# Rotating 96 images: 32 KB reads into four partitions each, twelve 8 KB slots per side, and one kind of group, in place of two kinds of groups with 8 and 16 KB packets

## The chip, the cores and the metric

The kernel runs on one core of a Trainium2 chip. The metric is the device time of one execution in microseconds (us). "Packet" is one entry of the trace's list of DMA packets; "MB" in my own sums of packets is 1,048,576 bytes.

## The reference

```python
def setup_inputs():
    batch, c, h, w = 32, 3, 256, 256
    return {"x": np.random.randn(batch, c, h, w).astype(np.float32)}

def reference(x):
    return np.rot90(x, k=1, axes=(-2, -1)).astype(np.float32)
```

There are 96 images of 256 x 256 float32 (256 KB each). Nothing is computed. 25.17 MB (decimal) are read, rotated in SBUF by transposes of 32 x 32 blocks on VectorE and by access patterns, and 25.17 MB are written.

## The kernel before

Sixteen images form a group of 4 MB. The first and the last group are of kind 1 (four transfers of 1 MB per side, 8 KB per partition), the four between are of kind 2 (two transfers of 2 MB per side, 16 KB per partition). SyncE issues the loads, ScalarE the stores, and three buffers per side hold three groups.

```python
G = 16
KINDS = [1, 2, 2, 2, 2, 1]
...
in_pool = ctx.enter_context(tc.tile_pool(name="in_pool", bufs=3))
out_pool = ctx.enter_context(tc.tile_pool(name="out_pool", bufs=3))

for g, kind in enumerate(KINDS):
    ...
    if kind == 1:
        ...                       # R = 8
        for s in range(4):
            nc.sync.dma_start(out=Sv[:, s], in_=xv[s])
        for s in range(4):
            ...
            nc.vector.transpose(dst, src)              # 128 x 2048
            nc.scalar.dma_start(out=ov[s], in_=Uv[:, s])
    else:
        ...                       # R = 16
        for b in range(2):
            nc.sync.dma_start(out=Sv[:, b], in_=xv[b])
        ...
        for q in range(R):
            nc.vector.transpose(dst[:, q], src[:, q])  # 128 x 512
        for a in range(2):
            nc.scalar.dma_start(out=ov[a], in_=Uv[:, a])
```

## Time and profile before

| | before |
|---|---|
| time, median | 124.06 us (3 runs, 124.03 to 124.07) |
| span of the profiled run | 122.2 us |
| bytes moved | 50.34 MB (decimal) |
| VectorE busy | 91.3 us (75%) |
| DMA queues q1 and q10 (their records show the loads in q1, the stores in q10) | 49.3% + 48.3% of 16 engines' span |

These are lines of the page of the profiled execution. The two rows of digits are busy tenths in 40 equal slices of the span; the row below them is what the DMA engines moved in each slice.

```profile
span 122.2 us, 170 instructions
DVE 91.3 (75%) x72; POOL 0.2 (0%) x4
...
DVE  0199999007999999999999990799999999092000
...
DMA  3999999999999999999999999999999999999993
GB/s 86 424 421 416 375 432 429 426 410 442 418 440 437 437 434 418 429 434 429 429 429 429 434 429 421 453 410 413 464 413 429 445 416 426 442 429 408 429 429 161
...
q1 hardware_dynamic: 2304, 25.17, 49.3%
q10 hardware_dynamic: 2304, 25.17, 48.3%
...
L65 DVE STREAM_TRANSPOSE U<-S 128x512 f32<-128x512 f32 x64 | 60.5, 1059 | 10.8 <-DMA S<-in_x_dram 7.1
```

The DMA row is at 9 in every slice but the first and the last, while VectorE (DVE) has gaps. The DMA engines bound this kernel.

The view by stretches of time, of the same run, in the middle (columns: stretch in us, its length, VectorE busy and instructions, GpSimd, granted clock, DMA share, GB/s):

```profile
30.00:60.00 30.00, 30.00 (x33) 0.00 (x0) 1.00 1.01 431
60.00:105.00 45.00, 40.12 (x34) 0.00 (x0) 1.00 1.01 430
```

The Trainium skill, "DMA: Bandwidth & Descriptors", section "Where 436 GB/s comes from", gives a ceiling of 16 x 32 B x 850 MHz = 435.2 GB/s. The middle runs within 1.2% of it.

### The profile page before, as it was taken

The page shows a single profiled execution, that of the slowest core. Times are in us where ns is not written, and L with a number is a line of the kernel's source. Part 1 is how long each engine was busy: PE and PEld are TensorE (multiplying, and loading weights), DVE is VectorE, ACT ScalarE, POOL GpSimd, SP SyncE. Part 2 cuts the span into 40 slices and gives each one's busy share as a digit, 9 for nine tenths or more (in the row PEclk, how much of TensorE's full clock was granted, in tenths as well). Part 3 has the DMA queues.
Part 4 walks back from the last instruction along what each step waited for, and adds up shares of the span by engine and source line. Part 5 has one row for each costly group of instructions (what it writes and reads, how often), then busy time and mean ns, then how long its engine had stood idle before and what let it go on. Part 6 is the DMA issues. An engine that isn't in the chain of part 4 may idle for free.

```text
span 122.2 us, 170 instructions
## 1 busy us (share of the span) xinstructions
DVE 91.3 (75%) x72; POOL 0.2 (0%) x4
## 2 busy tenths in 40 slices
DVE  0199999007999999999999990799999999092000
POOL 0000000000000000000000000000000000000000
DMA  3999999999999999999999999999999999999993
GB/s 86 424 421 416 375 432 429 426 410 442 418 440 437 437 434 418 429 434 429 429 429 429 434 429 421 453 410 413 464 413 429 445 416 426 442 429 408 429 429 161
DMA packets 4609, 50.34 MB, mean 412 GB/s; under 512 B 512, under 2 KB 512, under 8 KB 512
## 3 DMA queue, kind: packets, MB, share of 16 engines
q1 hardware_dynamic: 2304, 25.17, 49.3%
q10 hardware_dynamic: 2304, 25.17, 48.3%
q14 instruction: 1, 0.01, 0.0%
HBM read 25.17 MB, written 25.17 MB: 412 GB/s over the span
## 4 chain that ended last, share of the span: by engine, by line
DMA 61%; DVE 27%; issue 1%; SPq 1%
DMA S<-in_x_dram 46%; DVE U L65 24%; DMA out_dram<-U 16%; DVE U L49 3%; SPq L44 1%
## 5 line engine op out<-in xcount | busy, mean ns | idle before, releaser
L65 DVE STREAM_TRANSPOSE U<-S 128x512 f32<-128x512 f32 x64 | 60.5, 1059 | 10.8 <-DMA S<-in_x_dram 7.1
L49 DVE STREAM_TRANSPOSE U<-S 128x2048 f32<-128x2048 f32 x8 | 31.0, 3937 | 8.7 <-DMA S<-in_x_dram 8.7
L82 POOL MEMSET const-bfloat16-1.0<- 128x1 bf16 x1 | 0.1, 101 | 0.0
L82 POOL MEMSET const-uint8-127<- 128x1 uint8 x1 | 0.1, 101 | 0.0
L82 POOL MEMSET const-float32-0.0<- 128x1 f32 x1 | 0.1, 98 | 0.2 <-issue 0.2
L82 POOL MEMSET const-float32-1.0<- 128x1 f32 x1 | 0.1, 98 | 0.0
## 6 DMA issues: line engine op xcount, KB each, us to landing
S<-in_x_dram SPq DMA_DIRECT2D x8, 2048.0 KB, 21.1
out_dram<-U ACTq DMA_DIRECT2D x8, 2048.0 KB, 19.0
S<-in_x_dram SPq DMA_DIRECT2D x8, 1024.0 KB, 16.6
out_dram<-U ACTq DMA_DIRECT2D x8, 1024.0 KB, 16.1
```

The costliest lines, as they stand in the source:

```text
L44: nc.sync.dma_start(out=Sv[:, s], in_=xv[s])
L49: nc.vector.transpose(dst, src)
L65: nc.vector.transpose(dst[:, q], src[:, q])
L82: nc = _bacc.Bacc("TRN2", target_bir_lowering=False, num_devices=1)
```

## The change

The intent: fewer and longer packets on the load side (each read takes 32 KB of DRAM, which lands in four partitions of 8 KB), loads favoured over stores by that length, and one kind of group (8 images, one store of 2 MB in 16 KB packets). The buffers become twelve slots of 1 MB per side, the same 12 MB as before. The first load alone keeps 8 KB packets.

```diff
-    G = 16
-    KINDS = [1, 2, 2, 2, 2, 1]
+    RI = 8
+    FI = RI * W
+    MS = [2] * 12
+    NS, NU = 12, 12
+    FOLD = 32
...
+    xp = xf.rearrange("(n p f) -> n p f", p=P, f=FI)
+    xv = xf.rearrange("(n d f) -> n d f", n=N // 4, d=FOLD)
...
+    def load(dst, src):
+        nc.sync.add_instruction(mybir.InstDMACopy(
+            ...
+            ins=[nc.sync.lower_ap(src, opt=False)],
+            outs=[nc.sync.lower_ap(dst, opt=False)],
+            queue="qSPDynamicHW", mode="Copy"))
...
+        for b in range(m):
+            if n + b < 1:
+                nc.sync.dma_start(out=S[:, b], in_=xp[n + b])
+            else:
+                load(S[:, b], xv[n + b])
...
+            for r in range(RI):
+                nc.vector.transpose(dst[:, r], src[:, r])
...
+        nc.scalar.dma_start(
+            out=ov.rearrange("b (qk f) -> qk b f", f=RO * W), in_=U
+        )
```

More of the change, by code (lines that the diff above doesn't have):

```diff
@@ L20 @@
     P = 128
-    G = 16
-    KINDS = [1, 2, 2, 2, 2, 1]
-    assert len(KINDS) * G == N
-    F = G * H * W // P
-    fp32 = mybir.dt.float32
-    xf = x.rearrange("b c h w -> (b c h w)").rearrange("(g f) -> g f", g=N // G)
-    of = out.rearrange("b c h w -> (b c h w)").rearrange("(g f) -> g f", g=N // G)
-    in_pool = ctx.enter_context(tc.tile_pool(name="in_pool", bufs=3))
-    out_pool = ctx.enter_context(tc.tile_pool(name="out_pool", bufs=3))
-    for g, kind in enumerate(KINDS):
-        S = in_pool.tile([P, F], fp32, name="S")
-        U = out_pool.tile([P, F], fp32, name="U")
-        if kind == 1:
-            R = 8
-            Sv = S.rearrange("p (s f) -> p s f", s=4)
-            Uv = U.rearrange("p (s f) -> p s f", s=4)
-            xv = xf[g].rearrange("(s p f) -> s p f", s=4, p=P)
-            ov = of[g].rearrange("(s p f) -> s p f", s=4, p=P)
-            for s in range(4):
-                nc.sync.dma_start(out=Sv[:, s], in_=xv[s])
-            for s in range(4):
-                src = Sv[:, s].rearrange("p (r k q) -> p q r k", r=R, q=R)[:, ::-1, :, ::-1]
-                dst = Uv[:, s].rearrange("p (q k r) -> p q r k", q=R, r=R)
-                nc.vector.transpose(dst, src)
-                nc.scalar.dma_start(out=ov[s], in_=Uv[:, s])
-        else:
-            R = 16
-            Sv = S.rearrange("p (b f) -> p b f", b=2)
-            Uv = U.rearrange("p (a f) -> p a f", a=2)
-            xv = xf[g].rearrange("(b a qk f) -> b qk a f", b=2, a=2, f=F // 2)
-            ov = of[g].rearrange("(b a qk f) -> a qk b f", b=2, a=2, f=F // 2)
-            for b in range(2):
-                nc.sync.dma_start(out=Sv[:, b], in_=xv[b])
-            src = Sv.rearrange("p b (r k q) -> p q r k b", r=R, q=R)[:, ::-1, :, ::-1]
-            dst = Uv.rearrange("p a (q k r) -> p q r k a", q=R, r=R)
-            for q in range(R):
-                nc.vector.transpose(dst[:, q], src[:, q])
-            for a in range(2):
-                nc.scalar.dma_start(out=ov[a], in_=Uv[:, a])
@@ new lines @@
+    RI = 8
+    FI = RI * W
+    MS = [2] * 12
+    assert 4 * sum(MS) == N
+    NS, NU = 12, 12
+    FOLD = 32
+    fp32 = mybir.dt.float32
+    xf = x.rearrange("b c h w -> (b c h w)")
+    of = out.rearrange("b c h w -> (b c h w)")
+    xp = xf.rearrange("(n p f) -> n p f", p=P, f=FI)
+    xv = xf.rearrange("(n d f) -> n d f", n=N // 4, d=FOLD)
+    S_all = ctx.enter_context(tc.tile_pool(name="S", bufs=1)).tile([P, NS, FI], fp32, name="S_all")
+    U_all = ctx.enter_context(tc.tile_pool(name="U", bufs=1)).tile([P, NU, FI], fp32, name="U_all")
@@ new lines, in load @@
+    def load(dst, src):
+        nc.sync.add_instruction(
+            mybir.InstDMACopy(
+                name=nc.get_next_instruction_name(),
+                engine=mybir.EngineType.SP,
+                ins=[nc.sync.lower_ap(src, opt=False)],
+                outs=[nc.sync.lower_ap(dst, opt=False)],
+                queue="qSPDynamicHW",
+                mode="Copy",
+            )
+        )
+    n = s = u = 0
+    for m in MS:
+        if s + m > NS:
+            s = 0
+        if u + m > NU:
+            u = 0
+        RO = RI * m
+        S = S_all[:, s : s + m]
+        U = U_all[:, u : u + m].rearrange("p m f -> p (m f)")
+        for b in range(m):
[3 more added lines that the diff above has]
+                load(S[:, b], xv[n + b])
+        src = S.rearrange("p b (r k q) -> p r q k b", r=RI, q=RO)[:, :, ::-1, ::-1]
+        dst = U.rearrange("p (q k r) -> p r q k", q=RO, r=RI)
+        if m == 1:
+            nc.vector.transpose(dst, src[:, :, :, :, 0])
+        else:
+            for r in range(RI):
+                nc.vector.transpose(dst[:, r], src[:, r])
+        ov = of.rearrange("(n f) -> n f", f=P * FI)[n : n + m]
+        nc.scalar.dma_start(
+            out=ov.rearrange("b (qk f) -> qk b f", f=RO * W), in_=U
+        )
+        n += m
+        s += m
+        u += m
```

## The prediction

> **What bounds the kernel now.** The 16 DMA engines. 50.33 MB move; the rows by slice show DMA at 9 in all but the first and last slice, the table by stretches gives a DMA share of 1.00 to 1.02 and 424 to 433 GB/s from 15 to 119 us. VectorE is busy 75% (91.3 of 122.2 us) and its waits cost nothing. The packet records give 309 ns for 8 KB and 611 ns for 16 KB, in both directions: a slope of 27.1 bytes/ns per engine (434 GB/s for 16) plus about 7 ns per packet; a completion packet takes 9 ns. The Trainium skill, "DMA: Bandwidth & Descriptors", section "Where 436 GB/s comes from", puts a ceiling at 435; this trace agrees. Per engine: 128 x 309 + 128 x 611 ns + 32 x 9 ns = 118.05 us. The rest of the 122.2 us span: 2.5 us until the first packet, about 1.3 us of slow first packets and of skew between engines, 0.4 us after the last. The time is 1.85 us over the span.
>
> **What the change does.** Bytes are unchanged. Loads become one of 8 KB packets and 23 of 32 KB reads (if a read is one packet: 2 per engine and load, about 1.215 us each, estimated from the slope); the 12 stores of 2 MB keep 16 KB. Per engine: 2.5 + 46 x 1.215 + 96 x 0.611 + 36 x 0.009 = 117.3 us, which is 0.7 us less, all on the critical path. If instead each 8 KB write counts as a packet, 118.3 us, 0.25 us more.
>
> VectorE gets 96 transposes of 512 columns: at 1.059 us, 101.7 us instead of 91.3, off the path as long as it starts near 8 us (after two loads) and is fed. It then ends near 110 us, and the last 2 MB store (4.9 us) must still find a backlog of earlier stores; by my estimate, stepping the packets through both queues, it does, with 3 to 4 us to spare. A transpose over about 1.10 us would show in the time. The two patterns of before cost alike (3.94 us for four times the columns), so I expect 1.06 us.
>
> **Arbitration.** The same page, section "Queues, rings and completion order", says an engine alternates between queues packet by packet. The trace agrees: from 14 to 44 us, 16 KB loads against 8 KB stores, 2 MB loads and 1 MB stores both land every 7.3 us, a 2:1 split. So 32 KB reads against 16 KB stores give the loads two thirds: loads run ahead until slots or semaphores hold them, VectorE is never starved, stores have the backlog for the end. If the unit were the 8 KB write, loads would get one third, VectorE would starve from about 50 us, and some 6 us of DMA idle would stand before the last store: about 129 us.
>
> **Prediction: 123.4 us, range 122.5 to 125.2.** Faster by over 2%: 0.03; within 2%: 0.87; slower by over 2%: 0.10.
>
> **What would show it.** Load packets of 32 KB near 1.21 us; DMA at 9 in all middle slices, about 430 GB/s; 2 MB of loads landing for each 1 MB of stores early on; VectorE busy about 102 us, its waits only early; the chain of waits ending in stores that land back to back about 4.9 us apart; the load queue waiting mostly for stores.
>
> **What would make it wrong.** A 32 KB read off the slope; arbitration by write; [...] transposes slower than 1.10 us; or a gap before the last store. A gain over 2% needs over 434 GB/s, of which nothing here hints.

## More of the kernel before

Most executions of the kernel before lie within 0.3% of each other; verdicts use runs in the undisturbed state.

Look at the fifth slice, 12.2 to 15.3 us: 375 GB/s although the engines are busy.

## The result, and the profile after

The changed kernel takes 124.28 us (median of 4 runs, 124.15 to 124.31); the kernel before took 124.05 us in the same rounds (123.97 to 124.07). The ratio is 1.0018, 95% interval 1.0001 to 1.0036. A second submission of the same kernel (`again`, below) gave 124.32 us against 123.97 us, ratio 1.0026, 1.0007 to 1.0046. A ratio here is the mean time of one kernel's fast runs over that of the other's of the same rounds, so it is not quite the ratio of the medians. Executions over 1.5% slower than the fastest of the same kernel are left out of the means. The change makes the kernel 0.2 to 0.3% slower: both intervals lie just above 1. I had forecast 0.5% faster.

The lines of the page of the changed kernel that answer to those above:

```profile
span 122.5 us, 206 instructions
DVE 94.0 (77%) x96; POOL 0.2 (0%) x4
...
DVE  0039999999999999999949969950799995994000
...
DMA  4999999999999999999999999999899998999992
GB/s 112 498 417 439 417 407 342 364 428 428 428 433 455 455 444 401 455 401 465 436 385 492 385 407 428 449 417 498 364 444 417 439 498 353 428 428 428 428 428 96
...
q1 hardware_dynamic: 1248, 25.17, 49.3%
q10 hardware_dynamic: 1728, 25.17, 48.0%
...
L73 DVE STREAM_TRANSPOSE U_all<-S_all 128x512 f32<-128x512 f32 x96 | 94.0, 1161 | 17.6 <-DMA S_all<-in_x_dram 15.1
```

The load queue has 1248 packets in place of 2304, and yet it takes the same 49.3% of the span. The slow slices are now the seventh and eighth (18.4 to 24.5 us, 342 and 364 GB/s). The same stretches as before, from the view by stretches:

```profile
30.00:60.00 30.00, 30.00 (x32) 0.00 (x0) 1.00 1.02 437
60.00:105.00 45.00, 35.39 (x37) 0.00 (x0) 1.00 1.00 427
```

Over both stretches that is (30 x 437 + 45 x 427) / 75 = 431.0 GB/s, where before had 430.4. Long packets make a short stretch's figure coarse, because a packet is counted where it falls, so I also worked with the list of packets, each packet's bytes spread evenly over its record.

### A ledger: how far behind the ceiling

The table asks, at time T, how many us the bytes moved so far lie behind a stream of 435.2 GB/s that begins with the first packet at 1.75 us (1.72 to 1.75 us in these runs): T - 1.75 - bytes / 435.2 GB/s. A step between two columns is time lost there. The last three columns are times: the mean over 16 engines of their last completion, the last engine's completion, and the end of the span.

| T in us | 6 | 12 | 15 | 18 | 24 | 60 | 105 | 119 | mean end | last end | span |
|---|---|---|---|---|---|---|---|---|---|---|---|
| before | 0.97 | 1.12 | 1.67 | 1.72 | 1.81 | 2.32 | 2.85 | 3.06 | 120.49 | 121.07 | 122.22 |
| after | 0.75 | 0.82 | 0.92 | 1.01 | 1.89 | 2.25 | 2.81 | 2.94 | 120.36 | 121.13 | 122.50 |
| again | 0.90 | 0.98 | 1.07 | 1.16 | 1.86 | 2.23 | 2.78 | 2.91 | 120.33 | 121.12 | 122.50 |

Read it from left to right.

- Before loses 0.55 us between 12 and 15 us; the changed kernel loses 0.88 us (`again` 0.70) between 18 and 24 us. Both are the moment when the first store joins the loads.
- From 24 to 105 us before loses 1.04 us and the changed kernel 0.92 us. In this stretch longer packets gain 0.12 us. Another 0.08 us come between 105 and 119 us, where before stores in 8 KB packets and the changed kernel in 16 KB packets.
- At the mean end the changed kernel is 0.13 us ahead. Its last engine is 0.06 us behind, because its engines spread more (0.77 us from mean to last, where before has 0.58). From there to the end of the span it takes 1.38 us in place of 1.16. So the span is 0.28 us longer.

The prediction had 0.7 us of gain in the packets alone. The experiments ask where it went.

### The profile page after: what moved, and what is told of

Same layout as the page of the kernel before. It is cut to its first block, busy times and chain, and to the rows that moved or that the text cites. A ratio compares the mean times of both kernels' runs of the same rounds, so it can differ in the third digit from the quotient of the medians.

```text
span 122.5 us, 206 instructions
## 1 busy us (share of the span) xinstructions
DVE 94.0 (77%) x96; POOL 0.2 (0%) x4
## 3 DMA queue, kind: packets, MB, share of 16 engines
q1 hardware_dynamic: 1248, 25.17, 49.3%
## 4 chain that ended last, share of the span: by engine, by line
DMA 45%; DVE 40%; issue 4%; SPq 1%; DVEq 1%
DVE U_all L73 40%; DMA S_all<-in_x_dram 24%; DMA out_dram<-U_all 21%; DVEq L107 1%; SPq L40 1%; SPq L63 0%; DVEq L73 0%
## 5 line engine op out<-in xcount | busy, mean ns | idle before, releaser
L73 DVE STREAM_TRANSPOSE U_all<-S_all 128x512 f32<-128x512 f32 x96 | 94.0, 1161 | 17.6 <-DMA S_all<-in_x_dram 15.1
## 6 DMA issues: line engine op xcount, KB each, us to landing
out_dram<-U_all ACTq DMA_DIRECT2D x12, 2048.0 KB, 20.8
```

Source lines behind the costliest of these rows:

```text
L73: nc.vector.transpose(dst[:, r], src[:, r])
```

## The experiments

"Stretch" is the sum of what load packets last beyond the best of their length (309 ns for 8 KB, 611 for 16 KB, 1213 for 32 KB), divided by 16, in us per engine. It is counted where the first store joins, over one or two intervals of 3 us by when the packets end, unless said otherwise. Before has 0.51 us there, the changed kernel 0.87. The same kernel once more (`again`) has 0.67, and every run has one profile, so a difference below 0.2 us says nothing. "Joins" covers some time before the store's own packets: in the changed kernel the first store is issued at 16.0 us, the stretched loads start from 18 to 22 us, and the first store packet starts at 21.2 us.

### fold64: reads of 16 KB

```diff
-    FOLD = 32
+    FOLD = 64
```

> The changed kernel with 16 KB reads (each written to 2 partitions) in place of 32 KB. Question: the load packets of the changed kernel are 0.87 us per engine longer than the best 1213 ns where the first stores join (before: 0.51 us). Theory L (the length of the load packets sets it): about 0.5 us here. Theory S (the length of the first store's packets, 8 KB before and 16 KB after, sets it): still about 0.87 us. Packets alone cost 92 x 0.611 in place of 46 x 1.213 us, 0.4 us more. Time 124.3 us under L, 124.7 us under S. Loads and stores share evenly from the first store on.

Measured: correct; 126.18 us (126.13 to 126.27) against 124.08, ratio 1.0172 (1.0157 to 1.0188). The stretch is 0.79 us. So halving the load packet did not bring it down to before's 0.5: theory L fails, theory S fits within the spread. The time is higher than either theory said, and its DMA row says why:

```profile
DVE  0039999999999999966991994996699399299500
...
DMA  3999999999999999999999999999999999999293
```

Near the end the engines stand still (the 2 in the third slice from the end) before the last store. From 21.5 to 35 us, 172 load packets ran beside 177 store packets: turn by turn, so loads have half the bandwidth in place of 59%, VectorE gets its last data later, and the last store of 2 MB starts into an empty queue. Until then this kernel is not slower than the changed one: from 24 to 105 us its ledger loses 0.85 us (2.17 to 3.02), where the changed kernel loses 0.92. Reads of 32 KB moved no more bytes per us than reads of 16 KB did. What they bring is their share.

### fold128: ordinary loads of 8 KB

```diff
-            if n + b < 1:
+            if True:
```

> The changed kernel with ordinary loads of 8 KB packets, everything else kept. If an engine alternates queue by queue, packet by packet, loads get one third beside 16 KB stores: VectorE waits for loads from the middle on, and about 4 us of DMA idle stand before the last store; time 127.5 to 129.5 us. If the arbitration does not matter, 124.5 us. Stretch of loads where the first store joins: L about 0.25 us, S about 0.87 us.

Measured: correct; 129.92 us (129.78 to 130.13), ratio 1.0475 (1.0459 to 1.0490), 0.4 us outside the range. The stretch is 0.96 us, not 0.25: again S and not L. From 21.5 to 43 us, 382 load packets of 8 KB ran beside 372 store packets of 16 KB, so loads had a third. The waits of VectorE and the DMA row show the rest:

```profile
DVE  0049999999992399499399499399499599589600
...
DMA  4999999999999999999999999999999999893094
```

```profile
DVE U_all L73 <- DMA S_all<-in_x_dram: 22.0, 7, 8.2
DVE U_all L73 <- issue: 4.0, 2, 2.2
```

VectorE runs dry from about 38 us on (the 2 and the 3), and the engines are idle for most of a slice (the 0) before the last store. The Trainium skill, "DMA: Bandwidth & Descriptors", section "Queues, rings and completion order", says that an engine goes round its queues packet by packet; fold128, fold64 and before agree, at one packet for one (1.03, 0.97 and 0.99 load packets for each store packet while both queues had work).

The changed kernel seems to depart from this: from 21.5 to 32.5 us it has 80 load packets for 113 store packets, 59% of the bytes for loads and not two thirds. But if the 4-byte completion packets at the end of each transfer count as turns, it has 114 for 115, since a load of two packets per engine then takes three turns. The trace shows that they do count. Its list does not name the engine of a packet, but a record starts 3 or 4 ns before the end of the one that it follows, so the two can be matched by time. In the changed kernel from 22 to 32.5 us, all 80 load packets end where a store packet starts, and none within 40 ns of the start of a load packet. Of the 103 store packets that end there, 69 are followed by a load packet and 32 by a load's completion, most often with a store packet after it. fold64 has 205 turns for 193 counted this way (172 for 177 without completions); a difference of 12 is less than one turn for each of 16 engines, which the edges of the stretch can make. By this rule (an estimate) the changed kernel's loads get 2 x 32 KB for every 3 x 16 KB of stores, 57%.

fold128 also shows that the middle does gain up to 16 KB: from 24 to 105 us, without idle engines, it loses 1.20 us with 8 KB reads, where fold64 loses 0.85 and the changed kernel 0.92.

### m1first: first stores of 8 KB packets

```diff
-    MS = [2] * 12
+    MS = [1, 1] + [2] * 11
```

> The changed kernel, but its first two groups are of 4 images, so the first stores have 8 KB packets and the reads keep 32 KB. Stretch where the first store joins: theory S about 0.5 us, theory L about 0.87 us. The first store is issued near 10 us. Packets cost 0.06 us more. Time 123.9 to 124.0 us under S, 124.3 us under L. 37 transfers, so the last one still stands in an early one of the closing waits, and the 1.38 us tail stays.

Measured: correct; 124.26 us, but spread from 123.94 to 125.12; ratio 1.0035 (0.9992 to 1.0079), which decides nothing about the time. The profile does decide about the stretch: 0.50 us where the first store joins, with 32 KB reads all the same, and another 0.20 us at 23 to 26 us, after the first 16 KB store is issued at 21.1 us and before its first packet at 29.8 us. S fits. In all the ledger is at 1.74 us by 27 us, where the changed kernel is at 1.91: two steps cost less than one in this run (combo, below, which starts with the same stores, does not repeat it). The tail is 1.40 us, as expected.

### prime: a first transfer on ScalarE's queue at the start

```diff
+    scr = ctx.enter_context(tc.tile_pool(name="scr", bufs=1)).tile([16, 128], fp32, name="scr")
+    nc.scalar.dma_start(out=scr, in_=xf[: 16 * 128].rearrange("(p f) -> p f", p=16))
```

> The changed kernel with one transfer of 8 KB in all put on ScalarE's queue at the start. Theory C (the first transfer of a queue is what stretches the load packets: 2 to 5 us from its issue to its first packet): the stretch near the first store falls from 0.87 us to near nothing and the first store's packets start within 2 us of their issue; time about 123.4 us. Theories L and S: nothing changes, 124.3 us.

Measured: correct; 124.24 us (124.06 to 124.38), ratio 1.0015 (1.0000 to 1.0029). The stretch is 0.82 us. Theory C fails.

### b_kind2: the kernel before, with 16 KB packets from the start

```diff
-    KINDS = [1, 2, 2, 2, 2, 1]
+    KINDS = [2, 2, 2, 2, 2, 1]
```

> The kernel before with its first group made like its middle ones: first loads and first stores have 16 KB packets. Stretch of the load packets (sum over their best length, per engine) around the first store packets: theory S (store packet length sets it) 0.8 to 0.9 us in place of before's 0.51 us; theory L and any theory that blames the new loads or the new buffers: 0.5 us, as before. Packets alone cost 0.22 us less. 28 transfers, so the closing waits should cost 0.2 us more than in before (tail 1.36 us).

Measured: correct; 124.97 us (124.80 to 125.07), ratio 1.0070 (1.0040 to 1.0100). The stretch is 0.77 us: the old loads and the old buffers, with the longer first store packet, nearly reach the changed kernel's figure. S fits, and everything that blames the new loads or the new slots for the stretch fails. The tail is 1.32 us, near the 1.36 forecast for 28 transfers (see tail40). The stretch is not what makes this kernel 0.9 us slower: its first packet comes 0.40 us later than before's, and its last engine is 0.92 us behind the mean, where before has 0.58.

### step2k: the first store in 2 KB and then 14 KB packets

```diff
...
+        if n == 0:
+            nc.scalar.dma_start(out=ov[:, :, :512], in_=U[:, :512])
+            nc.scalar.dma_start(out=ov[:, :, 512:], in_=U[:, 512:])
...                               # every other store as before
```

> The changed kernel with its first store cut by columns: 2 KB packets first, then 14 KB. Theory S (length of one store packet): the stretch comes in two steps, at most 0.2 us where the 2 KB packets join, some 0.6 us more where the 14 KB packets follow. Rival B (a fixed number of bytes is read ahead, some 20 KB, in however many packets): 0.7 us or more in the first step. Rival C (any first store costs the same): about 0.5 us in the first step.

Measured: correct; 125.47 us in its one run, of unknown state. The 2 KB packets run from 20.9 to 26.2 us, between the load packets. Until 22 us the load packets are at most 69 ns above their best (22 ns in the mean; 27 to 33 when they were alone). From 22 to 24.5 us, still among the 2 KB packets and before the first 14 KB packet appears at 25.5 us, single load packets take up to 868 ns too long, about 0.5 us per engine together. So the stretch does come in two steps, and the second comes ahead of the long packets, as in the changed kernel the stretch comes ahead of the first store packet. B and C, as they were put down, fail; it is one run. It also answers a rival that no expectation names: that late stores, not long ones, stretch the loads. The 8 KB stores of before and m1first start at 13.6 to 13.8 us, the 16 KB stores of the other kernels so far at 20.4 to 33.6 us. Here short packets start at 20.9 us and cost next to nothing at first.

### unmixed: loads first, stores later (wrong result)

```diff
+    for n in range(24):
+        if n < 1:
+            nc.sync.dma_start(out=S_all[:, n], in_=xp[n])
+        else:
+            load(S_all[:, n % NS], xv[n])
+    for i in range(12):
+        u = 2 * (i % 6)
+        s = 10 - u
...                               # transposes and one store of 2 MB per i, as before
```

> Wrong result on purpose: all 24 loads of the changed kernel first, into the same 12 slots, then all transposes and stores. No load runs beside a store. If joining stores stretch the loads, no 32 KB packet after the first two loads takes over 1300 ns. If each of the four 8 KB writes of a read costs about 7 ns where nothing else runs beside, the packets take about 1240 ns here (1213 ns beside stores). If the 32 KB reads are stretched by themselves, packets of 1400 to 1900 ns appear here too.

Measured: wrong, one run. It did not come out as unmixed as planned: the first store joined at 50 us, while five loads were still to land. And there was no stretch at the join: load packets near their best plus 13 ns. (After the first two 32 KB loads the longest packet before the join is 1309 ns, just over the 1300 expected.) But while the loads ran alone each packet took about 1240 ns, and this sums up: 0.99 us per engine from the first 32 KB load to 50 us, 1.09 us in all. S alone, "store packets of 16 KB cost 0.8 us when they join", does not hold here.

The run also shows that 32 KB reads are not fast by themselves. The landings of successive 1 MB loads (means over the engines) lie 2445 to 2465 ns apart at first and 2485 ns apart from the seventh load on. The state of this run is unknown, and its last stores, too, land 4.91 us apart where the other runs have 4.86; but the changed kernel in a fast run has 2484 and 2485 ns for its loads just before the first store joins.

### unmixed128 and unmixed_k4: is it read-ahead?

The idea after unmixed (theory R): an engine reads ahead of what it writes, a longer store packet needs more of that, and it has to be built up once, in one stall when the store joins or bit by bit before.

```diff
-            load(S_all[:, n % NS], xv[n])
+            nc.sync.dma_start(out=S_all[:, n % NS], in_=xp[n])       # unmixed128
```

> Wrong result on purpose: the run unmixed with ordinary 8 KB loads. In unmixed the stores joined at 50 us with no stretch, against theory S. Theory R (read-ahead): an engine reads ahead of its writes; store packets need about their length more of it when they join, which the loads wait for; but 32 KB reads with four writes each (1240 ns of writing for some 1213 of reading) pile up read-ahead by 2% of the time they run alone, about 1 us by 50 us. Reads of 8 KB with one write each pile up none, so here the stretch must be back: 0.8 to 1.0 us per engine where the first store joins. Rival T (it only depends on how late, or on the addresses, in which unmixed differs): none here either.

Measured: wrong, one run. The stretch at the join (47 to 50 us) is 0.11 us, so R's expectation of 0.8 to 1.0 is refuted. What R had overlooked is that 8 KB packets, too, got longer while they ran alone: from about 17 us on they add 0.04 to 0.05 us per 3 us, 0.65 us per engine in all to the end of the loads when the start-up is left out. That is less than in the other runs with 16 KB stores. Their landings lie 2453 ns apart at first and settle at 2485 ns, the same as the 32 KB reads of unmixed. (b_kind2's loads of 2 MB in 16 KB packets, alone until 28 us, stay at 4863 ns, 2431 per MB. What slows the 1 MB loads after some 15 us I don't know.)

```diff
+    slots = [n % 10 for n in range(24)]
+    slots[4], slots[5] = 10, 11
...
-            load(S_all[:, n % NS], xv[n])
+            load(S_all[:, slots[n]], xv[n])                          # unmixed_k4, of unmixed
```

> Wrong result on purpose: the run unmixed (32 KB reads), with the first group's slots filled by loads 4 and 5, so that the first store joins near 30 us, between the changed kernel's 18 us (0.87 us of stretch) and unmixed's 48 us (none). Theory R: between, 0.5 to 0.7 us (0.87 less 2.2% of the 12 us more). Rival: all or nothing.

Measured: wrong, one run. Around the first store (26 to 35 us) 0.58 us of stretch are counted, 0.98 us from the first 32 KB load to there. It lies between, as R said. Later in this run the load queue stood empty for a while (about 45 us); when loads and stores met again at 53 us, 0.96 us of stretch came within 3 us. So lateness alone (rival T) does not take the stretch away.

Put side by side, from the first load's end to the end of the join, in us per engine: after 1.04, again 0.85, tail40 1.02, fold64 0.91, fold128 1.02, prime 0.99, step2k 0.83 (both steps), unmixed 1.09, unmixed_k4 0.98, b_kind2 0.78, unmixed128 0.65; with 8 KB stores, before 0.54 and m1first 0.57 (0.78 with its second step). combo, below, has 2.5 and fits no theory here. At the first join alone, the three kernels with 8 KB first stores (before, m1first, combo) have 0.50 or 0.51, and the seven with whole 16 KB ones that are not unmixed (after, again, fold64, fold128, prime, b_kind2, tail40) 0.67 to 0.96. For stores of 16 KB it is most often 0.8 to 1.1 us, paid at the join or in small parts before it. That is what a one-time build-up of read-ahead would look like, but unmixed128 does not fit in size, and no run shows the read side by itself. The mechanism is argued, not shown.

### tail40: where the last transfer stands in the closing waits

```diff
...                               # scr: a tile that nothing else uses
+            if 12 <= n + b < 16:
+                nc.sync.dma_start(out=scr[:, n + b - 12], in_=xf[: 16 * 128].rearrange("(p f) -> p f", p=16))
```

At the end SyncE waits for the eight DMA semaphores, two at a time, in a fixed order. Transfers take the eight in turn. With 32 transfers (before) the last one's semaphore is in the fourth wait. With 36 (after) it is in the first wait, and three more follow it, some 0.07 us apart.

> The changed kernel with four loads of 8 KB more in its middle, so that there are 40 transfers and the last store's semaphore stands in the last closing wait of SyncE, as in before, not in the first. From the last packet's end to the end of the span: 1.16 us as in before, not 1.38. The four cost 0.14 us of packets. Time 124.2 us, 0.05 us less than the changed kernel; the tail alone is the test.

Measured: correct; 124.62 us (124.47 to 124.92), ratio 1.0039 (1.0004 to 1.0075). The tail is 1.16 us, exactly as in before; in eight runs whose last transfer stands in the first wait (after, again, fold64, fold128, m1first, prime, step2k, b_kind2) it is 1.32 to 1.41 us. That settles 0.22 us. The time rose all the same: 0.97 us per engine of DMA idle stood before the last store. The four small loads moved the other transfers on to other semaphores, and loads came later; that the one caused the other is not shown.

### combo and again

```diff
-    MS = [2] * 12
+    MS = [1, 1] + [2] * 11
...
+            if 4 <= n + b < 7:
+                nc.sync.dma_start(out=scr[:, n + b - 4], in_=xf[: 16 * 128].rearrange("(p f) -> p f", p=16))
```

> A version that might beat both: the changed kernel with its first two groups of 4 images (first stores of 8 KB) and three loads of 8 KB more early on, so that the last of 40 transfers stands in the last closing wait. Tail 1.16 us in place of 1.38, stretch at the first store 0.5 and some 0.2 us later in place of 0.87, 0.17 us more packets. Together 0.2 us less than the changed kernel: 124.0 to 124.1 us, a tie with before.

Measured: correct; 125.91 us (five fast runs from 125.72 to 126.70, and one of 127.65, which the ratio leaves out), ratio 1.0159 (1.0130 to 1.0188). A clear miss. The tail is 1.20 us, and the first join 0.51 us plus 0.36. But the load queue was empty from 20.8 us, its last packet, to 21.7 us, when the next load had been issued. The first 16 KB store was issued then, too, and before its first packet at 26.8 us load packets were stretched by 1.65 us per engine within 3 us. The changed kernel also has an empty load queue, from 32.8 to 33.9 us, and no stretch after it, so an empty queue alone is not the cause. I did not find it.

> The changed kernel once more, to see how repeatable its profile is and to narrow the interval: 124.15 to 124.35 us, 0.1 to 0.3% above before; stretch where the first store joins 0.8 to 0.95 us; tail 1.35 to 1.40 us.

Measured: correct; 124.32 us (124.22 to 124.50), as expected. The stretch at the join is 0.67 us, below the expected range; but the start lost 0.15 us more, so that the ledger at 24 us is 1.86 us, where it was 1.89. Tail 1.38 us.

## Why the prediction was wrong

**The step that failed: "a slope of 27.1 bytes/ns per engine (434 GB/s for 16) plus about 7 ns per packet", taken as time that longer packets save.** The 7 ns came from the lengths of the records, and records of successive packets overlap. What an engine really needs is the distance from packet to packet, and the trace had it. The last four stores of before, of 8 KB packets and with nothing beside them, land 2453 ns apart: (2453 - 9) / 8 = 305.5 ns for a packet that is recorded as 309. The changed kernel's last stores land 4863 ns apart: (4863 - 9) / 8 = 606.7 ns for 16 KB, recorded as 611. The difference, 301.2 ns for 8 KB, is 27.2 bytes/ns, which is 435.2 GB/s for 16 engines and exactly the skill's ceiling; 4.3 ns remain per packet. My sum, redone with these (32 KB at 4 x 301.2 + 4.3 = 1209 ns, an estimate), says 117.05 us before and 116.63 after: 0.42 us in place of 0.7.

**Even this estimate was not met in full.** About 0.28 of the 0.42 us belong to the packets that start from 24 to 119 us (an estimate: their counts in the list times the costs above). The ledger has 0.12 us from 24 to 105 us and 0.08 after, 0.20 in all. The rest of the 0.42 us belongs before 24 us, where the next point finds nothing left of it. A 32 KB read did not cost its 1209 ns: from 24 to 105 us these reads last 1220 ns in the mean, 7 ns over the shortest, 0.21 us per engine; alone, the loads settled at 2485 ns per MB in 32 KB reads (unmixed) and in 8 KB packets (unmixed128) alike; beside stores, 16 KB reads (fold64) lost 0.85 us from 24 to 105 us, and 32 KB reads 0.92. The line of the profile that said so was the load queue's share: 49.3% before and after.

**"About 1.3 us of slow first packets and of skew" was carried over unchanged, and it did change.** By 24 us before had lost 1.81 us and the changed kernel 1.89 (1.86), although its start-up was 0.07 to 0.22 us cheaper. The join cost 0.88 (0.70) in place of 0.55 us. m1first, fold64, fold128, b_kind2 and step2k, one profile each, tie that to the store packets (unmixed and combo do not fit), 16 KB in place of 8 KB, a part of the change that I had costed as a saving. The spread of the engines at the end, 0.77 in place of 0.58 us, is measured and not explained.

**The tail was missed.** I put the first packet at 2.5 us and the end 0.4 us after the last one. It is 1.75 us and 1.16 us, and the 1.16 become 1.38 with 36 transfers. tail40 shows it.

**The terms together.** Against before, the changed kernel has +0.08 us by 24 us, -0.20 us from 24 to 119 us, +0.19 us from the spread of the engines and +0.22 us from the tail. That is 0.29 us, and the spans differ by 0.28. `again` has +0.05, -0.20, +0.21 and +0.22. So of the 0.7 us that I had forecast, 0.28 were never in the packets, some 0.08 went into longer records in the middle, and losses at the edges, of which I had costed none, outweigh the rest.

Point by point for the rest:

- A 32 KB read is one packet: right. 736 packets of 32 KB, the shortest 1213 ns, mean 1240.
- Arbitration by packet, loads ahead: right in kind, and it is what the 32 KB are good for; fold64 and fold128 cost 1.7% and 4.7% without them. The size was off, 59% of the bytes and not two thirds, because the completion packet of each load takes a turn as well (fold128).
- "VectorE is never starved", and waits only early: wrong, and harmless. The waits of VectorE of the changed kernel:

```profile
DVE U_all L73 <- DMA S_all<-in_x_dram: 15.1, 3, 8.0
DVE U_all L73 <- issue: 1.5, 1, 1.5
DVE U_all L73 <- DVE U_all L73: 1.0, 1, 1.0
```

  8.0 us of the 15.1 is the start, 5.1 us fall at 86 us. The load queue waits for stores, as I had said:

```profile
SPq L40 <- DMA out_dram<-U_all: 68.0, 7, 17.6
```

- VectorE busy 102 us: wrong, it is 94.0. I had multiplied by the mean record of 1059 ns, but these records overlap as well (64 x 1059 ns is 67.8 us, and the page had 60.5 busy). The distance from one transpose to the next was 0.945 us before and is 0.98 us after (94.0 / 96), while the mean record is 1161 ns. The Trainium skill, "Perfetto Trace Analysis", section "Optimizing Scalar/DVE Operations", says that an instruction's profiled latency is longer than its engine-busy time, because the write acknowledgement overlaps with the next instruction. This trace agrees that the records overlap (1059 ns recorded, 945 ns from one to the next); it does not show why. I had not applied it.
- No gap before the last store: right. The changed kernel's stores land 4.86 us apart at the end.
- The range held (124.28 in 122.5 to 125.2), and so did "within 2%". The direction was wrong.

## What to carry to other kernels

Take the cost of a packet or an instruction from the distance between successive ones where nothing else runs, not from the length of its record: with overlapping records, a few ns each become a gain that does not exist. When a kernel already moves within 1.2% of the ceiling through its middle, look at its edges, at what happens when stores first join the loads and after the last packet, since a change there outweighs what the middle can still give. And where two queues share the engines, packet lengths set their shares: 32, 16 and 8 KB reads beside 16 KB stores gave 124.3, 126.2 and 129.9 us.

## What the Trainium skill lacked or had wrong

- "DMA: Bandwidth & Descriptors", "Where 436 GB/s comes from": confirmed at 435.2 GB/s as the slope between packets of 8 and 16 KB. What the page says of a cost per packet stands under small descriptors and small transfers; for packets of 8 and 16 KB it gives none, and here it is 4.3 ns.
- The same page, "Queues, rings and completion order": packet by packet is confirmed, but the page calls 9 to 17 descriptors a typical packet. Here one read of 8, 16 or 32 KB was one turn (382 for 372, 172 for 177), and so was each completion of 4 bytes: 32 KB reads got 80 turns for 113 without completions, 114 for 115 with them. So the share of bytes follows the length of the reads, which the page doesn't say.
- The same page: nothing on what it costs when stores join loads: 0.5 to 0.55 us per engine with 8 KB store packets, 0.7 to 1 us with 16 KB (0.1 us or less at the join when loads had run alone for 48 us).
- The same page mentions loads whose reads are widened over several rows only for a limit on descriptors, and says nothing of their speed: 1 MB loads alone settled at 2485 ns in 32 KB reads and in 8 KB packets alike.
- No page: SyncE's closing waits cost some 0.07 us each after the last transfer, by where its semaphore stands (tail 1.16 or 1.38 us).
